# Row sums and weight sums of the third unit ordered behind the last token tile, and a Gelu given later, in the up projection of a ConvFFN

## The chip, the cores and the metric

The kernel runs on one core of one Trainium2 chip. The core has a matrix engine (PE), whose weight loads (PEld) overlap its products, and three engines for element-wise work: DVE (VectorE), ACT (ScalarE) and POOL (GpSimd). SP issues DMAs. Each of them takes its instructions from a queue of its own, in order, and waits at an instruction until what it needs is there. The metric is the time of one execution on the device in microseconds (us), smaller being better, as the median of several executions.

## The reference

A trunk of one encoder layer over 1024 tokens of width 1024: a token mixer, cross-attention into 256 memory tokens, and a gated ConvFFN, each added to its scaled input and normalised. The change lies where the cross-attention ends and the ConvFFN begins. Cut to that:

```python
def conv_ffn(h_in, w_up, b_up, w_dw, b_dw, w_down, b_down):
    h = h_in @ w_up + b_up                       # 1024 x 1024 times 1024 x 5632
    h = lax.conv_general_dilated(h, w_dw[:, None, :], ..., feature_group_count=2 * D_FF) + b_dw   # width 3 over tokens
    g, u = jnp.split(h, 2, axis=-1)              # D_FF = 2816 each
    y = jax.nn.gelu(g, approximate=False) * u
    return y @ w_down + b_down

h = layer_norm(DN_ALPHA * h + memory_xattn(h, ...), ln2_w, ln2_b)
h = layer_norm(DN_ALPHA * h + conv_ffn(h, ...), ln3_w, ln3_b)
```

## The kernel before

**Units.** The up projection is cut into 22 units (`NFF`). Unit v holds 128 columns of g and the 128 columns of u that are multiplied with them. Each unit's product with the tokens is made by a scheme with seven products instead of eight (Winograd's form of Strassen's), on quarters: weights A11, A12, A21, A22 with the sums S1 to S4, tokens B11, B12, B21, B22 with the sums T1 to T4. All operands are split into a high and a low 16-bit part, so that one product is three matmuls for each of four slices (`mm3`, lines 224 to 226), 12 matmuls of 128 x 512, and a unit has 7 x 12 = 84.

**Weights of a unit** (class `Units`, lines 1505 to 1576). `load` (L1517) brings 1 MB into one of two buffers `ur`; units 0 and 1 have buffers of their own. `bound` sums the absolute values of each row on ACT (L1524, output to the scratch tile `junk`, of which there is one) and casts the sums on DVE (L1525). `scale` sends them through PE (L182, tile `mx`) and five small steps on DVE (L183, L174 to L176, L1533) to a power of two. `sums` makes S1 to S4 on POOL (L1547 to L1550). `split_A` and `split_S` scale and split on ACT (L203) and DVE (L204). `prep` is sums, split_A and split_S as a generator with four steps. Once `split_A` and `sums` are done, the buffer `ur` is free for the next load.

**Tokens.** `out_d` ends the cross-attention for one token tile of 128 tokens: an eviction (L1480), the norm (`ln_tile`: statistics L237 and L239, L241, a power of -1/2 on POOL at L242, for the last tile the normalising step L244), the store to DRAM (L1483). `to_B` then transposes the tile on PE (L1381), evicts it on ACT (L1284) and DVE (L1286), and for every second tile forms T1 to T4 and B22 and splits them (`pair`: ACT at L1411, DVE at L1412, for some on POOL). The last tile's `to_B` runs after the products A11 B11 and A12 B21 of unit 0, which need nothing of it, are given; those of unit 1 are given behind it. Then comes `units.bound(2, junk)`.

**The loop of the up projection** (lines 1779 to 1829), for each v: load unit v+3; weight sums of unit v+2; product A11 B11 of unit v and its eviction m1 (L1709); scale of unit v+2; A12 B21 and C11; A22 T4 and C21 of unit v-1; split_A; S2 T2 and u2; the first half of `post` for unit v-2 in the order of the loop (depthwise convolution: L1683 on ACT, L1684 and L1685 on DVE); the row sum of unit v+3; S1 T1; S4 B22 and C12 of unit v-1; the split of the sums; S3 T3, u3 and C22; then the second half of `post` (Gelu L1689 on ACT, product with u L1690 on DVE, store of y L1691, its largest absolute values by a sum L1692 on ACT); and a survey of a piece of w_down (DMA L1727, row sum L1728). The PSUM bank X of a unit takes A11 B11, is evicted by m1, and takes S2 T2 on top, so PE must wait for m1 before S2 T2.

**Order.** The text gives a rank, not the order itself. When the program is built, the order of each engine's queue is worked out from simulated times: of the instructions that are ready then, the one that stands first in the text goes first (line 2001). `with tc.issue_after(x.ins):` adds an order: what is given inside the block comes behind x in the queue, where both are on the same engine. It adds no wait between engines.

Of the kernel before, what the change touches and what calls it, by code (L numbers as in the profile page):

```python
# [13 lines left out]
AF = mybir.ActivationFunctionType  # L14
OP = mybir.AluOpType
# [35 lines left out]
def run(gen):  # L51
    for _ in gen:
        pass
# [3 lines left out]
def encoder(ctx, tc, I, out):  # L57
    nc = tc.nc
    V, A, G, T, S = nc.vector, nc.scalar, nc.gpsimd, nc.tensor, nc.sync
# [19 lines left out]
    def bank(name):  # L79
        key = "mem" if name == "tk" else name  # L80
        turn[key] = turn.get(key, -1) + 1
        tag = SET[name][turn[key] % len(SET[name])]
        return pp.tile([128, 512], F32, name=name, tag=tag, bufs=NB[tag])
# [23 lines left out]
    mhalf = consts.tile([128, 4], F32, name="mhalf")  # L107
# [122 lines left out]
        V.tensor_tensor(lo, src, hi.bitcast(F32), OP.subtract)  # L230


    def ln_tile(r, w_t, b_t, small, late=False, hold=None, eps=EPS, parts=1, pieces=2):
        st = small.tile([128, pieces, 6], F32, name="lnst", tag=f"lnst{pieces}", bufs=3 if pieces == 2 else 1)
        with (tc.issue_after(hold.ins) if hold is not None else nullcontext()):
            for i in range(pieces):
                V.bn_stats(st[:, i, :], r[:, i * D // pieces:(i + 1) * D // pieces])  # L237
        mv = small.tile([128, 2], F32, name="lnmv", bufs=3)
        V.bn_aggr(mv, st)  # L239
        rs = small.tile([128, 2], F32, name="lnrs", bufs=3)  # L240
        V.tensor_scalar(rs[:, 0:1], mv[:, 1:2], eps, None, op0=OP.add)  # L241
        G.tensor_tensor(rs[:, 0:1], rs[:, 0:1], mhalf[:, 0:1], OP.pow)  # L242
        if late and w_t is None:
            return V.tensor_scalar(r, r, mv[:, 0:1], rs[:, 0:1], op0=OP.subtract, op1=OP.mult)  # L244
        if late:
            for i in range(parts):
                c = slice(i * D // parts, (i + 1) * D // parts)
                V.scalar_tensor_tensor(r[:, c], r[:, c], mv[:, 0:1], w_t[:, c], op0=OP.subtract, op1=OP.mult)
                V.scalar_tensor_tensor(r[:, c], r[:, c], rs[:, 0:1], b_t[:, c], op0=OP.mult, op1=OP.add)
            return  # L250
        n = V.tensor_scalar(rs[:, 1:2], mv[:, 0:1], rs[:, 0:1], -1.0, op0=OP.mult, op1=OP.mult)
        A.activation(r, r, AF.Identity, scale=rs[:, 0:1], bias=rs[:, 1:2])
        if w_t is None:
            return n
        a = V.tensor_tensor(r, r, w_t, OP.mult)
        G.tensor_tensor(r, r, b_t, OP.add)
        return a
# [1016 lines left out]
    with ExitStack() as cb_:  # L1274
# [26 lines left out]
        todo = [0, 2, 1, 3, 4, 6, 5, 7]  # L1301
        rs, hT, probs, rq, holds, stores = {}, {}, {}, [], [], []
# [71 lines left out]
        def to_B(r, tt):  # L1374
# [33 lines left out]
            T1, T2, T3, T4 = t12[:, 0], t12[:, 1], t34[:, 0], t34[:, 1]  # L1408
            def pair(n, src):
                h, l = (t[:, :, o] for t in Bop[n])  # L1410
                A.activation(h, src, AF.Copy)  # L1411
                (G if n in ("B22", "T3") and tt not in todo[-2:] else V).tensor_tensor(l, src, h, OP.subtract)  # L1412

            V.tensor_tensor(T1, e12, B1[:, 0], OP.subtract)
            V.tensor_tensor(T2, e22, T1, OP.subtract)
# [2 lines left out]
            V.tensor_tensor(T3, e22, e12, OP.subtract)  # L1418
            if tt not in todo[-2:]:
                pair("B22", e22)  # L1420
            pair("T3", T3)
            V.tensor_tensor(T4, B1[:, 1], T2, OP.subtract)
            pair("T4", T4)
            if tt in todo[-2:]:
                pair("B22", e22)

        Vo = [[], []]
        for i in range(4):
# [149 lines left out]
        units = Units()  # L1578
# [40 lines left out]
        junk = ur.tile([128, 2048], BF, name="junk")  # L1619

        def prod(ps, v, a, b, first, last):
            (ah, al), (bh, bl) = units.got[v][a], Bop[b]
            for k in range(4):
                mm3(ps, ah[:, k, :], al[:, k, :], bh[:, k, :], bl[:, k, :], first and k == 0, k == 3, skip=True)
# [21 lines left out]

        with rtx:

            X, Z, W = {}, {}, {}
            for v in range(2):  # L1650
                X[v], Z[v] = bank("z"), bank("z")
                if rq and v == 1:
                    to_B(*rq.pop(0))
                prod(X[v], v, "A11", "B11", True, False)
                prod(Z[v], v, "A12", "B21", True, True)
                W[v] = bank("z")
            run(units.split_S(1))
            units.bound(2, junk)

# [3 lines left out]
        with ExitStack() as cE:  # L1665
# [109 lines left out]
                sy[g] = scale_of(ysum[:, :NG] if g == 0 else ysum[:, NG:], 14)  # L1775

            take(0, "m1")
            loaded, posts = None, []
            for v in range(NFF):
                loaded = units.load(v + 3) or loaded  # L1780
                pr = units.prep(v + 2)
                next(pr, None)
                if v > 1:
                    X[v], Z[v], W[v] = bank("z"), bank("z"), bank("z")
                    prod(X[v], v, "A11", "B11", True, False)
                if v > 1:
                    take(v, "m1")
                units.scale(v + 2)
                if v > 1:
                    prod(Z[v], v, "A12", "B21", True, True)  # L1790
# [28 lines left out]
                prod(X[v], v, "S3", "T3", False, False)  # L1819
                take(v, "u3")  # L1820
                take(v, "C22")
                if posts:
                    run(posts.pop())
                if v > 0:
                    posts.append(post(v - 1))
                if v < NFF - 2:
# [2 lines left out]
                        survey_down(NFF - 1 - v // 10)  # L1829

            v = NFF - 1
            ps = {}
            w_pair(1, 0)
            for tt in range(5):
# [13 lines left out]
        with ExitStack() as cF:  # L1848
# [39 lines left out]
            rs = {}  # L1888
# [9 lines left out]
            for tt in range(NT):  # L1898
# [10 lines left out]
                n = 256 if last else 512  # L1909
# [95 lines left out]
```

## Time and profile before

| | |
|---|---|
| median of 3 executions | 1481.03 us (1478.51 to 1482.34) |
| profiled execution, its time | 1481.55 us |
| its span, first to last instruction | 1479.8 us |
| PE busy | 1435.1 us |
| mean granted clock of PE | 0.993 |
| DVE, ACT, POOL busy | 1034.1, 821.5, 553.5 us |

A row of a list in order of time has the start in us from the span's first instruction, the duration, the engine, the line of the kernel, the operation, output and inputs by tile name with their sizes, and in brackets the idle time of the engine before it with what ended it. Matmuls overlap: one of 128 x 512 lasts 0.38 us, and the next may start 0.22 us after it. A row of the stretches has the bounds, the length, and for PE, PEld, DVE, ACT and POOL the busy time with the number of instructions, then the granted clock of PE as a share of full speed, the busy share of the DMA engines and GB/s.

### The profile page before, as it was taken

Reading aid. Unit: us, or ns where it says so; the run is one execution under the profiler, and the core shown is the slowest. Engines: PE = TensorE matmul, PEld = TensorE weight load, DVE = VectorE, ACT = ScalarE, POOL = GpSimd, SP = SyncE. Lnnn points to the kernel's source line nnn. Section 1 sums busy time; section 2 is a strip of 40 time slices with the busy share of each in tenths; the row PEclk is TensorE's granted clock in tenths of the full one; section 3 lists DMA queues with packets and bytes.
Section 4 is the critical chain, followed back from the end, with each engine's and each line's share of the span. In section 5 each row is a group of like instructions: output and inputs, shape, how many; then the busy total and the mean of one; then the engine's idle time right before and its main releaser. Section 6 shows DMA issues by size and latency. Waiting matters only on the chain. (4 is left out here: it accounts for less than half of the span.)

```text
span 1479.8 us, 21506 instructions
## 1 busy us (share of the span) xinstructions
PE 1435.1 (97%) x7996; PEld 844.2 (57%) x7996; DVE 1034.1 (70%) x1950; ACT 821.5 (56%) x1385; POOL 553.5 (37%) x440
## 2 busy tenths in 40 slices
PE   8999899999999999999999899999999999999998
PEld 6998776456766777774444444444444444444445
DVE  7867866535777778589658878787888888707424
ACT  5765465565563576424455777777777767403001
POOL 4452356502334766055114153343444400300543
PEclk9999999999999999999999999999999999999999
DMA  8845654214654644643343333233322437603121
GB/s 302 318 180 198 184 190 153 84 50 129 159 147 152 206 142 141 256 148 72 86 100 86 116 143 128 114 114 128 114 114 113 144 142 242 228 28 110 47 71 58
DMA packets 116383, 208.61 MB, mean 141 GB/s; under 512 B 40627, under 2 KB 69555, under 8 KB 112950
## 3 DMA queue, kind: packets, MB, share of 16 engines
q1 hardware_dynamic: 115984, 206.47, 42.0%
q8 instruction: 63, 1.03, 0.3%
q0 software_dynamic: 144, 0.49, 0.2%
q14 instruction: 42, 0.34, 0.1%
q10 hardware_dynamic: 150, 0.27, 0.0%
HBM read 154.15 MB, written 45.15 MB: 135 GB/s over the span
## 5 line engine op out<-in xcount | busy, mean ns | idle before, releaser
L1547 POOL TENSOR_TENSOR wraw<-ur 128x512 f32<-128x512 f32 x20 | 42.5, 2125 | 213.6 <-issue 193.0
L225 PE MATMUL dn<-wlo,yp 128*128 128x512 f16 (+1 forms) x284 | 105.1, 370 | 0.0
L224 PE MATMUL dn<-whi,yp 128*128 128x512 f16 (+1 forms) x284 | 104.9, 370 | 0.0
L226 PE MATMUL dn<-whi,yp 128*128 128x512 f16 (+1 forms) x284 | 104.4, 370 | 0.0
L1684 DVE SCALAR_TENSOR_TENSOR cbuf<-C,wdw,cbuf 128x1024 f32<-128x1024 f32 x44 | 71.4, 1623 | 30.8 <-ACT cbuf L1683 30.4
L225 PEld LDWEIGHTS <-whi 128*128 128x128 f16 x540 | 52.8, 98 | 58.0 <-issue 5.9
L226 PEld LDWEIGHTS <-wlo 128*128 128x128 f16 x540 | 52.8, 98 | 56.7 <-DVE wlo L204 1.3
L224 PEld LDWEIGHTS <-whi 128*128 128x128 f16 x540 | 52.8, 98 | 54.7 <-issue 1.7
L204 DVE SCALAR_TENSOR_TENSOR wlo<-wraw,us,whi 128x1024 f16<-128x1024 f32 (+1 forms) x48 | 62.8, 1325 | 21.3 <-ACT whi L203 21.3
L242 POOL TENSOR_TENSOR lnrs<-lnrs,mhalf 128x1 f32<-128x1 f32 x32 | 23.5, 735 | 127.4 <-DVE lnrs L241 90.2
L1685 DVE SCALAR_TENSOR_TENSOR cbuf<-C,wdw,cbuf 128x1024 f32<-128x1024 f32 x44 | 69.8, 1587 | 1.1
L1683 ACT ACTIVATE cbuf<-C,bdw,wdw 128x1024 f32<-128x1024 f32 x44 | 54.4, 1235 | 17.8 <-DVE C L1721 17.2
L1524 ACT ACTIVATE junk<-ur 128x2048 bf16<-128x2048 f32 x20 | 38.2, 1912 | 40.1 <-DMA ur<-in_w_up_dram 40.1
L203 ACT ACTIVATE whi<-wraw,us 128x1024 f16<-128x1024 f32 (+1 forms) x48 | 51.1, 1102 | 16.0 <-DVE us L176 15.8
L225 PEld LDWEIGHTS <-yp 128*128 128x128 f16 x370 | 36.2, 98 | 39.9
L224 PEld LDWEIGHTS <-yp 128*128 128x128 f16 x370 | 36.2, 98 | 39.8
L226 PEld LDWEIGHTS <-yp 128*128 128x128 f16 x370 | 36.2, 98 | 39.7
L224 PE MATMUL tk<-whi,Bo 128*128 128x256 f16 (+1 forms) x192 | 52.6, 274 | 2.9 <-DVE stage L204 2.9
L224 PE MATMUL tk<-whi,Be 128*128 128x256 f16 (+1 forms) x192 | 52.6, 274 | 0.9 <-DVE stage L204 0.8
L225 PE MATMUL tk<-wlo,Be 128*128 128x256 f16 (+1 forms) x192 | 52.4, 274 | 0.8 <-DVE wlo L204 0.8
L226 PE MATMUL tk<-whi,Bo 128*128 128x256 f16 (+1 forms) x192 | 52.5, 274 | 0.0
L226 PE MATMUL tk<-whi,Be 128*128 128x256 f16 (+1 forms) x192 | 52.5, 274 | 0.0
(555 smaller groups left out, 4802.2 us busy)
## 6 DMA issues: line engine op xcount, KB each, us to landing
ur<-in_w_up_dram SPq DMA_DIRECT2D x20, 1024.0 KB
sv<-in_w_down_dram SPq DMA_DIRECT2D x22, 512.0 KB
y<-cbuf SPq DMA_DIRECT2D x22, 512.0 KB
ur<-y SPq DMA_DIRECT2D x11, 1024.0 KB
wraw<-in_w_down_dram SPq DMA_DIRECT2D x22, 512.0 KB
r<-h SPq DMA_DIRECT2D x11, 512.0 KB
wraw<-in_w_tok_dram SPq DMA_DIRECT2D x10, 512.0 KB
wr<-in_w_xk_dram SPq DMA_DIRECT2D x8, 512.0 KB
```

Source lines behind the costliest of these rows:

```text
L203: A.activation(hi, src, AF.Copy, scale=s)
L204: return V.scalar_tensor_tensor(lo, src, s, hi, op0=OP.mult, op1=OP.subtract)
L224: T.matmul(ps, lh, rh, start=first, stop=False, skip_group_check=skip)
L225: T.matmul(ps, lh, rl, start=False, stop=False, skip_group_check=skip)
L226: return T.matmul(ps, ll, rh, start=False, stop=last, skip_group_check=skip)
L242: G.tensor_tensor(rs[:, 0:1], rs[:, 0:1], mhalf[:, 0:1], OP.pow)
L1524: A.activation(junk, self.raw[v], AF.Abs, accum_out=l1)
L1547: G.tensor_tensor(S1, A21, A22, OP.add)
L1683: A.activation(c, C[:, 1:SEQ + 1], AF.Identity, scale=wdw[:, 1, j:j + 1], bias=bdw[:, j:j + 1])
L1684: V.scalar_tensor_tensor(c, C[:, 0:SEQ], wdw[:, 0, j:j + 1], c, op0=OP.mult, op1=OP.add)
L1685: V.scalar_tensor_tensor(c, C[:, 2:SEQ + 2], wdw[:, 2, j:j + 1], c, op0=OP.mult, op1=OP.add)
```

## The change

Two parts, all in order; the instructions and their operands stay as they are.

First, the power of the last token tile's norm and the two instructions that split its T3 are remembered. The row sum and cast of the third unit (v = 2) are put behind those two, and the first step of its `prep`, the four weight sums on POOL, behind the power.

Second, the second half of `post` (Gelu to the row sum of y) is no longer given at the end of a round but in the next one, behind the load, the weight sums, the first product and its eviction m1, and ahead of `scale`. After the last round it is run once more.

```diff
+    power = [None]
...
-        G.tensor_tensor(rs[:, 0:1], rs[:, 0:1], mhalf[:, 0:1], OP.pow)
+        power[0] = G.tensor_tensor(rs[:, 0:1], rs[:, 0:1], mhalf[:, 0:1], OP.pow)
...
-                A.activation(h, src, AF.Copy)
-                (G if n in ("B22", "T3") and tt not in todo[-2:] else V).tensor_tensor(l, src, h, OP.subtract)
+                a = A.activation(h, src, AF.Copy)
+                b = (G if n in ("B22", "T3") and tt not in todo[-2:] else V).tensor_tensor(l, src, h, OP.subtract)
+                return a, b
...
-            pair("T3", T3)
+            ends = pair("T3", T3)
...
+            return ends
...
+            powered = power[0]
...
-                    to_B(*rq.pop(0))
+                    ends = to_B(*rq.pop(0))
...
-            units.bound(2, junk)
+            with tc.issue_after(ends[0].ins), tc.issue_after(ends[1].ins):
+                units.bound(2, junk)
...
-            loaded, posts = None, []
+            loaded, posts, ending = None, [], ()
...
-                next(pr, None)
+                with (tc.issue_after(powered.ins) if v == 0 else nullcontext()):
+                    next(pr, None)
...
                     take(v, "m1")
+                run(ending)
                 units.scale(v + 2)
...
-                if posts:
-                    run(posts.pop())
+                ending = posts.pop() if posts else ()
                 if v > 0:
                     posts.append(post(v - 1))
...
             v = NFF - 1
+            run(ending)
```

## The prediction

> **What bounds the kernel now.** First the page's busy line, then busy time by stretch, then the waits of PE from the start of the up projection on: a row says who waited for whom, us in total, how often, the longest.
>
> ```profile
> PE 1435.1 (97%) x7996; PEld 844.2 (57%) x7996; DVE 1034.1 (70%) x1950; ACT 821.5 (56%) x1385; POOL 553.5 (37%) x440
> ```
> ```profile
> 838.00:849.00 11.00, 6.43 (x23) 2.37 (x22) 11.00 (x28) 9.44 (x17) 0.00 (x0) 0.84 0.19 54
> ...
> 1003.00:1155.00 152.00, 148.73 (x691) 67.05 (x690) 122.59 (x141) 113.25 (x132) 63.14 (x32) 1.00 0.30 115
> ```
> ```profile
> 1200.00:1250.00 50.00, 50.00 (x236) 23.08 (x234) 46.55 (x54) 36.46 (x39) 0.00 (x0) 1.00 0.62 211
> ```
> ```profile
> PE z L224 <- ACT C L1709: 3.3, 8, 0.9
> PE z L224 <- ACT C L1713: 1.6, 3, 0.8
> ...
> PE z L225 <- DVE TX1l L1412: 0.6, 1, 0.6
> PE mx L182 <- DVE am L1525: 0.4, 1, 0.4
> ```
>
> PE is busy 97% of the span, so a change pays only where PE stands still. Two places of the up projection matter. Between 838 and 849 us PE is busy for 6.43 of 11.00 us and its clock falls to a mean of 0.84: 4.57 us idle. Later it loses 3.3 us in eight short waits for L1709, the first eviction of a unit ("m1"). From 1200 us on it is full, so time won earlier should reach the end.
>
> The order of PE through the first place:
>
> ```profile
> 835.85 1.06 PE L1381 MATMUL tp<-ident,r 128*128 128x128 f32 x8
> ...
> 838.26 0.38 PE L226 MATMUL z<-Bh,unitA 128*128 128x512 f16 x1
> 839.67 0.22 PE L182 MATMUL mx<-identb,am 128*128 128x128 bf16 x1 [1.03 <-ACT spare L1284]
> 841.43 0.22 PE L182 MATMUL mx<-identb,am 128*128 128x128 bf16 x1 [1.54 <-DVE us L183]
> ...
> 844.91 0.58 PE L225 MATMUL z<-TX1l,unitYh 128*128 128x512 f16 x1 [0.65 <-DVE TX1l L1412]
> ...
> 847.40 0.38 PE L225 MATMUL z<-TX1l,unitYh 128*128 128x512 f16 x1
> ...
> 848.27 0.38 PE L226 MATMUL z<-TX1l,unitYh 128*128 128x512 f16 x1
> ```
>
> At 835.85 come the transposes of the last token tile, at 838.26 the last product that needs none of it, and only at 844.91 do the products on the sums T1 to T4 run on. Behind the stall six matmuls take 847.40 - 844.91 = 2.49 us, 0.415 each, the next four (848.27 - 847.40) / 4 = 0.22 each: 6 x 0.195 = 1.2 us lost to a half clock. Loss: 4.57 + 1.2 = 5.8 us, and about 5 x (0.38 - 0.22) = 0.8 us more, since a broken row of matmuls counts each last one at its full 0.38: 6.6 us.
>
> **Why the last tile is late.** DVE, POOL and ACT:
>
> ```profile
> 808.50 0.21 DVE L241 TENSOR_SCALAR lnrs<-lnmv,sc 128x1 f32<-128x1 f32 x1
> 809.38 0.21 DVE L251 TENSOR_SCALAR lnrs<-lnmv,lnrs 128x1 f32<-128x1 f32 x1 [0.66 <-POOL lnrs L242]
> ...
> 827.83 0.21 DVE L239 BATCH_NORM_AGGREGATE lnmv<-lnst 128x2 f32<-128x12 f32 x1
> 830.72 0.16 DVE L1525 CAST am<-l 128x1 bf16<-128x1 f32 x1 [2.69 <-ACT junk L1524]
> 830.79 0.20 DVE L241 TENSOR_SCALAR lnrs<-lnmv,sc 128x1 f32<-128x1 f32 x1
> ...
> 833.67 2.04 DVE L244 TENSOR_SCALAR r<-r,lnmv,lnrs 128x1024 f32<-128x1024 f32 x1
> ...
> 844.18 0.68 DVE L1412 TENSOR_TENSOR TX1l<-spare,TX1l 128x512 f16<-128x512 f32 x1
> ```
> ```profile
> 828.82 1.28 POOL L1547 TENSOR_TENSOR wraw<-ur 128x512 f32<-128x512 f32 x1 [8.85 <-DMA ur<-in_w_up_dram]
> ...
> 832.52 1.00 POOL L242 TENSOR_TENSOR lnrs<-lnrs,mhalf 128x1 f32<-128x1 f32 x1
> 833.48 1.27 POOL L1550 TENSOR_TENSOR wraw<-ur,wraw 128x512 f32<-128x512 f32 x1
> ```
> ```profile
> 828.69 1.91 ACT L1524 ACTIVATE junk<-ur 128x2048 bf16<-128x2048 f32 x1 [4.07 <-DMA ur<-in_w_up_dram]
> ...
> 832.65 1.93 ACT L1524 ACTIVATE junk<-ur 128x2048 bf16<-128x2048 f32 x1
> ...
> 843.51 0.63 ACT L1411 ACTIVATE TX1l<-spare 128x512 f16<-128x512 f32 x1
> ...
> 846.16 1.58 ACT L203 ACTIVATE unitYl<-ur,us 128x1536 f16<-128x1536 f32 x1
> ```
>
> Each engine works off its queue in order. ACT stands 4.07 us before the third unit's row sum (L1524, 828.69), which waits for a DMA, while evictions of the last token tile but one lie behind it. DVE stands 2.69 us at the cast L1525 that waits for the same row sum, with L241 of the last tile's norm behind it. On POOL the power L242 lies behind three weight sums of the third unit and starts only at 832.52. So the norm's last step L244 starts at 833.67, though its statistics were ready at 828.04.
>
> **The change, first part.** The two edges put unit 2's row sum (ACT) and cast (DVE) behind the last tile's T3 split, and its first weight sums (POOL) behind the last power; unit 3's row sum writes the same tile junk and stays behind. No instruction is added or left out. Queued behind the moved ones are, on ACT, the T4 split and the weight splits; on DVE, the steps from scale product to scale; on POOL, the clearing of the C buffers' edges, which the first convolution reads long after.
>
> Norm: 828.04 plus the 0.88 us that another tile shows from L241 through POOL to the next DVE step (808.50 to 809.38) is 828.9, not 833.67: 4.75 us earlier. The transposes can then run about 831 instead of 835.85, and in front of them ACT has lost the 4.07 us stand and two row sums (1.91 and 1.93). From the end of the transposes (835.85 + 1.06 = 836.9) to the end of the first T split needed (844.18 + 0.68 = 844.9) passed 8.0 us. Kept at 8.0 it ends at 840; PE has products until 838.5, so 1.5 us of stall is left. Shortened by what no longer lies in it, none is. PE wins 6.6 - 1.5 = 5.1 at least, 6.6 at most if the order of PE uses the earlier tile; I take 6.2, nearer the upper end, because ACT's 1.2 us (836.9 to the tile's evictions at about 838.1) and the two scale products mx both leave that stretch.
>
> What is late next: unit 2's weights. T3's split on ACT ended at 843.51 + 0.63 = 844.14; 6 us earlier it is 838.1. Behind it come two row sums, 2.1 us each with their read of the sum (1.91 + 0.19), then the split of unit 2 (L203): 842.3 instead of 846.16, 3.9 us earlier. It frees the buffer for unit 4's load, and the two rows of buffers make unit 5's load, row sum and scale product wait in turn. That product already held PE up:
>
> ```profile
> 866.55 0.23 PE L182 MATMUL mx<-identb,am 128*128 128x128 bf16 x1 [0.37 <-DVE am L1525]
> ```
>
> PE, 6.2 us earlier, meets a weight chain that is only 3.9 earlier, with no slack there: it gives back 2.3 us. Bounds for this term: nothing, if the scale product is placed later in PE's queue, and all but the chain's own gain. First part: 6.2 - 2.3 = 3.9 us, between 0 and 6.6, and below 0 by the rival named slower.
>
> **Second part.** The Gelu, its product, the store of y and the row sum L1692 are given after the next unit's load, weight sums, first product and m1, and after the survey row sum L1728. Instructions stay the same; SP gets the weight load ahead of the store of y, which costs nothing, as the load waits for its buffer and not for the queue. One of the eight rounds:
>
> ```profile
> 1038.38 0.76 ACT L1715 ACTIVATE C<-z,bup,us 128x512 f32<-128x512 f32 x1
> 1041.15 1.06 ACT L1689 ACTIVATE cbuf<-cbuf 128x1024 f32<-128x1024 f32 x1 [2.01 <-DVE cbuf L1685]
> 1042.11 0.77 ACT L1709 ACTIVATE C<-z,bup,us 128x512 f32<-128x512 f32 x1
> ```
> ```profile
> 1031.93 0.38 PE L226 MATMUL z<-Bh,wlo 128*128 128x512 f16 x1
> 1032.14 0.38 PE L224 MATMUL z<-TX1l,unitYl 128*128 128x512 f16 x1
> ...
> 1034.73 0.38 PE L224 MATMUL z<-Bh,whi 128*128 128x512 f16 x1
> ...
> 1036.46 0.38 PE L226 MATMUL z<-Bh,wlo 128*128 128x512 f16 x1
> ...
> 1042.93 0.38 PE L224 MATMUL z<-TX1h,whi 128*128 128x512 f16 x1 [0.42 <-ACT C L1709]
> ```
> ```profile
>   DVE cbuf L1685: 32.2, 17
> ```
>
> The last row is ACT's idle time before Gelu: 32.2 us in 17 rounds. Here m1 could run from 1036.8 on, but lies behind Gelu, which stands 2.01 us for the convolution; PE waits 0.42. With m1 in front it runs at 1039.1 in that idle time and the wait is gone: 3.3 us over the eight rounds is the most. The other bound is nothing: who comes first is settled when the program is built, by what is ready then (PE takes three products of the next unit, leaves them at 1032.14 for the earlier unit's, and returns at 1034.73). In these rounds Gelu may thus lead because it was ready first in that reckoning, and a later place in the text need not turn that; then this part does not do what it says. Below nothing it goes only where m1, put in front, holds Gelu up: its product ends at 1036.8, 4.3 us before Gelu can start (1041.15), so not here. I take a third of the upper bound, 1.1 us, as the reckoning is not to be seen in the trace and one row speaks for each side.
>
> **Sum.** 3.9 + 1.1 = 5.0 us off the span of 1479.8: 1474.8. Around the span lie 1481.55 - 1479.8 = 1.75 us, and the profiled execution is 0.5 above the median of 1481.03: 1474.8 + 1.75 - 0.5 = 1476.0 us.
>
> **Rivals.**
>
> *Both parts in full* (0.18): the scale products fall where they cost nothing and m1 leads in all eight rounds: 6.6 + 3.3 = 9.9, 1471.1 us. For it: after each Gelu the next split then comes at once, which shortens the weight chain too. Against it: unit 5's product had no slack.
>
> *The weight chain swallows it* (0.20): the chain, not PE, sets the pace (Gelu, split, load, row sum, convolution, Gelu; from 1003 to 1155 us PE idles 3.27 us on it), and what PE wins at 849 it waits out later. With a chain only 0 to 2 us earlier: 1479 to 1481.
>
> *POOL blocks DVE* (0.10). L244 took 2.04 us where POOL's L1550 ran until 833.48 + 1.27 = 834.75; another step of its kind and size took 0.74:
>
> ```profile
> L1859 DVE TENSOR_SCALAR vec<-vec,sc x1: 741/741/741, 1220.7 to 1220.7; 128x1024 f32<-128x1024 f32 x1
> ```
>
> 834.75 to L244's end at 835.71 is 0.96, so it stood for about 1.1. Four weight sums now start right behind the power, at the very time of L244 and of the sums T1 to T4. One or two blocks of 1.3 us on the last tile's path leave 1477 to 1478.5. The Trainium skill, SBUF — State Buffer, section "Who interferes with whom", states such a lock: DVE's two-port modes share a port pair with GpSimd, and whichever issues first holds the other off for its whole instruction. By that rule this rival comes true at least once; the trace agrees with the lock (2.04 against 0.74).
>
> *Slower* (0.10): third unit late. If the last tile comes earlier by a, the split of unit 2 starts at 844.14 - a + 4.2 = 848.3 - a against 846.16. Below a = 2.2 us the chain is later than before, and each later unit with it, through the buffers. At a = 0, an order on PE that keeps the transposes where they were and scale products that hold PE, this is 2.2 us and up to 2 x 2.1 us for PE at the two scale products: 1481 + 2.2 to 6.4 = 1483 to 1487.
>
> **How the numbers follow.** Forecast 0.42 (1474 to 1478.5 alone), the rivals 0.18, 0.20, 0.10, 0.10. Range 1471 to 1483: it leaves out the lower half of the full case and most of the slower one. The measurement of this kernel can tell 0.3%, 4.4 us: faster means under 1476.6. From the forecast 0.29, from the full case 0.18: 0.47; slower 0.07 from the slower case and a reshuffled order; same 0.46.
>
> **What would show it.** Norm: L244 starts near 829 to 830 and the transposes before 833. Stall: PE's idle time between the last Bh product of unit 1 and steady T products under 1.5 us, the clock at 1.00. Chain: split of unit 2 (L203) at 842 to 843, and a wait of PE for L1525 of about 2 us near 860. Second part: L1709 in front of L1689 in the rounds around 1003 to 1155, PE's waits for L1709 below 3.3 us. The prediction is wrong if PE's queue keeps the scale products ahead of the T products, if the Gelu order is turned everywhere, or if a later stage turns out to lack the slack that its full PE suggests.

## The result, and the profile after

| | before | after |
|---|---|---|
| median of 10 executions each | 1481.43 us (1478.46 to 1484.69) | 1486.71 us (1482.88 to 1488.42) |
| profiled execution, its span | 1479.8 us | 1486.1 us |
| first product of the up projection to the first of the down projection | 409.34 us | 415.32 us |

The changed kernel is slower: ratio 1.0041 [1.0029, 1.0053]. The forecast was 1476.0 us with a range from 1471 to 1483; sign and range were both wrong.

The third row comes from the starts of two matmuls in the list of PE in order of time, for before (1236.33 - 826.99) and for after (1242.55 - 827.23):

```profile
826.99 0.38 PE L224 MATMUL z<-Bh,unitYh 128*128 128x512 f16 x1
...
1236.33 0.38 PE L224 MATMUL dn<-whi,yp 128*128 128x512 f16 x1
```
```profile
827.23 0.38 PE L224 MATMUL z<-Bh,unitYh 128*128 128x512 f16 x1
...
1242.55 0.38 PE L224 MATMUL dn<-whi,yp 128*128 128x512 f16 x1
```

Behind it lie 243.5 us in both, so all that was lost (5.98 us in these two executions) was lost in the up projection. Where that projection starts differs by up to 4.3 us between the profiled executions of this study; times of different kernels are therefore compared from its first product on.

Lines of the changed kernel are numbered 2 to 6 higher: L246 is the norm's last step, L1413 and L1414 are the splits of `pair`, L1417 to L1425 the sums T1 to T4, L1286 and L1288 the evictions of a transposed tile, L1528 and L1529 row sum and cast, L1551 to L1554 the weight sums, L1715, L1719, L1721 and L1725 the evictions m1, u2, u3 and C21. First the stretch of the old stall, then the waits of PE from 826 to 1180 us, in the changed kernel, and behind them one row of the same waits in the kernel before:

```profile
838.00:849.00 11.00, 7.19 (x27) 2.66 (x26) 8.80 (x17) 10.16 (x18) 0.00 (x0) 0.84 0.25 77
```
```profile
PE z L224 <- ACT C L1715: 4.6, 11, 1.5
PE z L224 <- ACT TX1l L1413: 3.7, 1, 3.7
PE z L224 <- ACT C L1721: 3.4, 2, 2.7
PE z L224 <- ACT C L1725: 1.5, 1, 1.5
PE z L224 <- ACT C L1719: 1.1, 1, 1.1
PE z L224 <- DVE C L1723: 1.1, 1, 1.1
```
```profile
PE z L224 <- ACT C L1715: 0.9, 2, 0.6
```

The stall is still there: 3.81 us idle instead of 4.57, the clock at 0.84 as before, now in one piece of 3.7 us instead of several. New are the waits for C21 (L1725) and C22 (L1723). The waits for u3 (L1721, L1715 before) have grown from 0.9 to 3.4 us and those for m1 from 3.3 to 4.6 us. Those for u2 (L1719, L1713 before) have shrunk from 1.6 to 1.1 us, but lie at another place, behind unit 2's split.

PE's idle time plus what the half clock cost (each interval between two starts above 0.25 us, less 0.216, the interval at full clock), in us from the first product of the up projection:

| stretch | before | after |
|---|---|---|
| 0 to 30 us, with the old stall | 4.63 + 1.20 | 4.83 + 0.76 |
| 30 to 110 us | 1.74 + 0.07 | 5.27 + 1.75 |
| 110 us to the end | 4.42 + 0.27 | 5.27 + 0.21 |

The sums are 12.3 and 18.1 us; their difference, 5.8 us, is the 5.98 us that were lost, within 0.2 us. Of the 4.83 us in the first row, 1.10 us are the wait for u2 at 856.24; at the old stall itself PE lost 3.73 + 0.76 us, 1.3 us less than before. So there are two questions: why the first stretch won next to nothing, and what lost 5.2 us in the second.

**The first stretch.** DVE, POOL, ACT and PE of the changed kernel:

```profile
829.71 1.75 DVE L246 TENSOR_SCALAR r<-r,lnmv,lnrs 128x1024 f32<-128x1024 f32 x1 [0.44 <-POOL lnrs L244]
...
833.06 1.75 DVE L1418 TENSOR_TENSOR ysum<-r,ysum 128x512 f32<-128x512 f32 x1
834.74 1.76 DVE L1421 TENSOR_TENSOR ysum<-r 128x512 f32<-128x512 f32 x1
```
```profile
829.65 1.26 POOL L1551 TENSOR_TENSOR wraw<-ur 128x512 f32<-128x512 f32 x1
830.88 1.71 POOL L1553 TENSOR_TENSOR wraw<-ur 128x512 f32<-128x512 f32 x1
...
834.34 1.60 POOL L1554 TENSOR_TENSOR wraw<-ur,wraw 128x512 f32<-128x512 f32 x1
```
```profile
832.20 0.63 ACT L1413 ACTIVATE whi<-r 128x512 f16<-128x512 f32 x1 [2.27 <-DVE r L1288]
834.85 0.63 ACT L1413 ACTIVATE TX1h<-ysum 128x512 f16<-128x512 f32 x1 [2.02 <-DVE ysum L1418]
...
838.27 2.18 ACT L1286 ACTIVATE spare<-tp,wb 128x128 f32<-128x128 f32 x6
...
843.20 0.66 ACT L1413 ACTIVATE TX1l<-spare 128x512 f16<-128x512 f32 x1
...
851.87 1.57 ACT L203 ACTIVATE unitYl<-ur,us 128x1536 f16<-128x1536 f32 x1
```
```profile
834.14 1.04 PE L1383 MATMUL tp<-ident,r 128*128 128x128 f32 x8
...
842.36 0.58 PE L224 MATMUL z<-TX1l,unitYh 128*128 128x512 f16 x1 [3.73 <-ACT TX1l L1413]
...
850.72 0.22 PE L182 MATMUL mx<-identb,am 128*128 128x128 bf16 x1
...
856.24 0.38 PE L224 MATMUL z<-TX1l,unitYh 128*128 128x512 f16 x1 [1.10 <-ACT C L1719]
```

The norm starts at 829.71, some 4 us earlier than before, as forecast. But the four weight sums now start with it, and while they run, the norm takes 1.75 us, and so do two of DVE's sums for tile 6, T2 and T3, instead of 0.68 each. (Tile 6 is the last token tile but one.) ACT splits tile 6 in front of the last tile's evictions and waits for DVE four times: 2.27 us for an eviction of DVE's (L1288) that stands behind the norm, 2.02 us for T2, and less for T3 and T4. The transposes of the last tile come at 834.14 without a wait: PE's queue has them behind other products. The last tile's evictions thus begin at 838.27 (838.13 before), and the split of T3 at 843.20 (843.51 before): not 6 us earlier but 0.3. The row sum of the third unit follows it, its scale product stands in PE's queue behind products of the last tile and runs at 850.72 without any wait of PE, and unit 2's split starts at 851.87 instead of 846.16. Behind that split stands the eviction u2, for which PE waits at 856.24.

**The second stretch.** SP, ACT, DVE and PE of the changed kernel, and behind it SP and ACT of the kernel before:

```profile
855.53 0.33 SPq L1521 DMA_DIRECT2D ur<-in_w_up_dram  x1
...
864.33 0.33 SPq L1521 DMA_DIRECT2D ur<-in_w_up_dram  x1
```
```profile
871.45 1.91 ACT L1528 ACTIVATE junk<-ur 128x2048 bf16<-128x2048 f32 x1 [4.55 <-DMA ur<-in_w_up_dram]
...
873.35 0.76 ACT L1725 ACTIVATE C<-z,bup,us 128x512 f32<-128x512 f32 x1
...
882.45 1.56 ACT L203 ACTIVATE unitYh<-ur,us 128x1536 f16<-128x1536 f32 x1
...
897.14 1.06 ACT L1695 ACTIVATE cbuf<-cbuf 128x1024 f32<-128x1024 f32 x1 [2.67 <-DVE cbuf L1691]
898.11 1.56 ACT L203 ACTIVATE unitA<-ur,us 128x1536 f16<-128x1536 f32 x1
...
901.65 0.77 ACT L1721 ACTIVATE C<-z,bup,us 128x512 f32<-128x512 f32 x1
```
```profile
873.48 0.16 DVE L1529 CAST am<-l 128x1 bf16<-128x1 f32 x1 [4.86 <-ACT junk L1528]
```
```profile
902.47 0.38 PE L224 MATMUL z<-TX1h,unitYl 128*128 128x512 f16 x1 [2.68 <-ACT C L1721]
...
903.66 0.63 PE L226 MATMUL z<-TX1h,unitYl 128*128 128x512 f16 x1
```
```profile
850.08 0.33 SPq L1517 DMA_DIRECT2D ur<-in_w_up_dram  x1
...
859.09 0.33 SPq L1517 DMA_DIRECT2D ur<-in_w_up_dram  x1
```
```profile
864.30 1.91 ACT L1524 ACTIVATE junk<-ur 128x2048 bf16<-128x2048 f32 x1 [1.18 <-DMA ur<-in_w_up_dram]
...
871.05 1.56 ACT L203 ACTIVATE unitYh<-ur,us 128x1536 f16<-128x1536 f32 x1
```

The loads of units 4 and 5 are issued 5.4 and 5.2 us later, since they wait for buffers. The row sum of unit 5 stands in ACT's queue in front of C21, so ACT stands 4.55 us (1.18 before) and DVE, at the cast, 4.86; PE waits for C21. Unit 4's split slips from 871.05 to 882.45. Near 897 Gelu waits 2.67 us for the convolution, three splits follow, and only then comes u3, for which PE stands 2.68 us; the 0.63 us at 903.66 is the half clock behind it.

**The second part** of the change did nothing. Up to their line numbers, the instructions of all five engines stand in the same order in the kernel before and in the kernel before with this part alone (run 1).

### The profile page after: what moved, and what is told of

It is laid out like the page before. It is cut to its first block, busy times and chain, and to the rows that moved or that the text cites. A ratio compares the mean times of both kernels' runs of the same rounds, so it can differ in the third digit from the quotient of the medians.

```text
span 1486.1 us, 21505 instructions
## 1 busy us (share of the span) xinstructions
PE 1439.8 (97%) x7996; PEld 846.8 (57%) x7996; DVE 1041.1 (70%) x1950; ACT 821.7 (55%) x1385; POOL 558.2 (38%) x440
## 4 chain that ended last, share of the span: by engine, by line
PE 61%; DVE 13%; DMA 9%; ACT 9%; issue 4%; POOL 2%; SPq 1%; DVEq 0%; ACTq 0%; POOLq 0%
DMA ur<-in_w_up_dram 5%; PE dn L225 5%; PE dn L226 5%; PE dn L224 5%; PE S L224 4%; PE S L225 4%; PE S L226 4%; PE tk L224 2%; PE tk L225 2%; PE tk L226 2%; DVE cbuf L1690 2%; DVE cbuf L1691 2%; PE cl L224 2%; PE cl L225 2%; PE cl L226 2%
## 5 line engine op out<-in xcount | busy, mean ns | idle before, releaser
L1551 POOL TENSOR_TENSOR wraw<-ur 128x512 f32<-128x512 f32 x20 | 40.7, 2036 | 208.3 <-issue 172.2
L1528 ACT ACTIVATE junk<-ur 128x2048 bf16<-128x2048 f32 x20 | 38.3, 1913 | 37.7 <-DMA ur<-in_w_up_dram 37.6
L225 PE MATMUL tk<-wlo,Bo 128*128 128x256 f16 (+1 forms) x192 | 53.7, 280 | 0.0
L224 PE MATMUL tk<-whi,Be 128*128 128x256 f16 (+1 forms) x192 | 52.6, 274 | 0.1
```

The source lines that it names most:

```text
L224: T.matmul(ps, lh, rh, start=first, stop=False, skip_group_check=skip)
L225: T.matmul(ps, lh, rl, start=False, stop=False, skip_group_check=skip)
L1528: A.activation(junk, self.raw[v], AF.Abs, accum_out=l1)
L1551: G.tensor_tensor(S1, A21, A22, OP.add)
```

## The experiments

Ratios are to the kernel before, with their 95% intervals. The last column is the length from the first product of the up projection to the first of the down projection in the one profiled execution, 409.34 us for the kernel before; it need not agree with the ratio, which is of medians.

| run | ratio | us |
|---|---|---|
| the change | 1.0041 [1.0029, 1.0053] | 415.32 |
| 1 second part alone | 1.0002 [0.9993, 1.0011] | 409.83 |
| 2 row sum and cast late, POOL as before | 1.0018 [1.0009, 1.0027] | 412.32 |
| 3 weight sums behind the power, row sum as before | 1.0012 [1.0003, 1.0022] | 412.60 |
| 4 row sum early, weight sums behind the power | 1.0002 [0.9994, 1.0011] | 411.43 |
| 5 row sum late, weight sums behind tile 6's T4 | 1.0047 [1.0035, 1.0058] | 413.86 |
| 6 row sum early, weight sums behind tile 6's T4 | 1.0014 [1.0006, 1.0023] | 410.92 |
| 7 kernel before, third unit's load not held back | 1.0036 [1.0024, 1.0047] | 412.13 |
| 8 kernel before, unit 2's split held back | 1.0005 [0.9994, 1.0015] | 410.70 |
| 9 row sum early, weight sums behind the last T4 | 1.0010 [0.9999, 1.0021] | 410.95 |
| 10 row sum late, weight sums behind the last T4 | 1.0024 [1.0015, 1.0033] | 412.24 |
| 11 row sum early, POOL as before | 1.0004 [0.9994, 1.0014] | 409.63 |
| 12 the change, unit 5's row sum put back | 1.0009 [0.9996, 1.0022] | 410.71 |
| 13 kernel before, unit 5's row sum put back | 1.0001 [0.9988, 1.0013] | 410.78 |
| 14 run 10, unit 5's row sum put back | 0.9990 [0.9978, 1.0003] | 409.51 |
| 15 run 9, unit 5's row sum put back | 0.9992 [0.9977, 1.0006] | 408.48 |

**Taking the change apart: runs 1 to 3.** Run 1 is the second part alone, run 2 the edges on ACT and DVE alone, run 3 the edge on POOL alone, each in the kernel before:

```diff
-                if posts:
-                    run(posts.pop())
+                ending = posts.pop() if posts else ()
...
+                run(ending)
                 units.scale(v + 2)
```
```diff
-            units.bound(2, junk)
+            with tc.issue_after(ends[0].ins), tc.issue_after(ends[1].ins):
+                units.bound(2, junk)
```
```diff
-                next(pr, None)
+                with (tc.issue_after(powered.ins) if v == 0 else nullcontext()):
+                    next(pr, None)
```

> The second part alone (Gelu half of post given a round later in the text; no edge on the row sums or weight sums). Theory A (the third unit's row sums come too late behind the T3 split, so its weight split, and every later load through the two buffers, slips by 5 to 6 us) and theory B (POOL's weight sums, now at the same time as the last tile's DVE steps, block them): both expect no change, 1481.4 within 2 us, the Gelu still ahead of m1 in the later rounds and PE's waits for m1 at 3.3 us. Theory C (the Gelu's new place is what costs): 1485 to 1488, most of the loss.

> Only the edges on the row sum and the cast of the third unit; the weight sums on POOL stay ahead of the power, Gelu as before. Theory A: slower by 4 to 7 us (1485 to 1488), the first split of unit 2 on ACT near 852 instead of 846.2. Theory B: within 2 us of before, since POOL's sums lie where they lay. Theory C: as before.

> Only the edge of the weight sums behind the power on POOL. Theory A: not slower, 1478 to 1482, as the row sums stay early and unit 2's split at 846 or before. Theory B: slower by 3 to 6 us (1484 to 1487), with DVE's steps L244, T2 and T3 of the last tiles at 1.7 us instead of 0.7. Theory C: as before.

The second part is out: level. Each half of the first part is a loss, 0.18% and 0.12%, both smaller than the theories expected (2.7 us for 4 to 7, 1.8 us for 3 to 6). Run 2 has the new waits 30 to 110 us after the start (2.59 us and a half clock of 1.68); run 3 has none there (0.20 us) but loses 9.2 us instead of 5.8 in the first stretch.

**Early places: runs 4 and 11.** The row sum is put only behind tile 6's last eviction on ACT, the cast behind the last norm. Run 4 keeps the edge on POOL, run 11 leaves it out.

```diff
+        normed = holds[-1]
         to_B(*rq.pop(0))
+        evicted6 = evicted[0]
...
-            with tc.issue_after(ends[0].ins), tc.issue_after(ends[1].ins):
+            with tc.issue_after(evicted6.ins), tc.issue_after(normed.ins):
                 units.bound(2, junk)
```

> The first part with its edges moved forward: the third unit's row sum behind the last ACT eviction of the last token tile but one (not behind the T3 split), its cast behind the last tile's normalising step, the weight sums behind the power as in the change; Gelu as before. Theory A: the loss is gone; the row sums fill ACT's idle time between 829 and 838, unit 2's split starts at 846 or before, 1476 to 1481. Theory B: the weight sums collide as in the changed kernel, so still slower than before by 3 to 6 us.

> Row sum and cast in the early place (behind tile 6's last eviction on ACT and behind the last norm), the weight sums on POOL without an order of their own, so that they may run ahead of the last power as in the kernel before. Theory: the norm of the last tile is late as before (832 to 833), the sums T1 to T4 run without POOL beside them but the evictions of tile 6 no longer wait for the third unit's load; unit 2's split at 846 to 848. Level with the kernel before: 0.999 to 1.001. If the order of POOL was a loss by itself in the early place, this run is faster than that one by 1 to 2 us.

Both are level, neither is faster. With the row sum early, the second stretch is like that of before (1.37 and 0.87 us lost). The new waits thus come with the late row sum, but the runs do not yet say by what.

**Without POOL beside tile 6: runs 5 and 6.** A small copy on POOL reads tile 6's T4 (`summed`) and the weight sums come behind it. Run 5 keeps the late row sum, run 6 has the early one.

```diff
+            summed[0] = T4[:, 0, 0:1]
...
-            powered = power[0]
+            held = small.tile([128, 1], F32, name="held")
+            with tc.issue_after(power[0].ins):
+                powered = G.tensor_copy(held, summed[0])
```

> The first part of the change with one small POOL copy more, which reads the last sum T4 of the last token tile but one and stands between the power and the weight sums: the sums start some 6 us later, after DVE's steps of that tile. Theory B (POOL's weight sums hold DVE up on the path): DVE's normalising step falls from 1.75 to about 0.75 us and T2 and T3 of that tile from 1.75 to 0.7, the evictions of the last tile on ACT start at 835 to 836 instead of 838.3, the split of unit 2 near 849 instead of 851.9, and 2 to 4 of the 6 us come back: 1482 to 1484. If the lock only fills time that the ACT queue would lose anyway: no change, 1486 to 1488.

> Row sum and cast of the third unit moved forward as in the run before (behind the last tile but one's evictions and the normalising step) and the small POOL copy ahead of the weight sums. Theories A and B together: both costs are gone, the last tile's evictions start before 835, PE's stall before the T products falls from 4.6 us to 1 to 3 us, 1475 to 1479, faster than before. If something else holds the last tile: 1480 to 1482, like the run without the copy.

In run 5 the sums of tile 6 take 0.7 us, and the last tile's evictions start at 834.4; but the weight sums now lie beside the last tile's own sums, which take 1.0 to 1.8 us, and nothing is won. POOL's hold (its weight sums lengthening DVE's steps) had only been moved by one tile. Run 6, expected to be faster, is slower by 0.14%: it has no new waits in the second stretch (0.49 us), but loses 7.5 us in the first.

**The load instead of the row sum: run 7.** The kernel before without the order that keeps the third unit's load behind the last store of h.

```diff
-        with tc.issue_after(stores[-1].ins):
-            units.load(2)
+        units.load(2)
```

> The kernel before, without the edge that puts the third unit's load behind the store of the last token tile but one; nothing of the change. Both loads then leave SP some 10 us earlier and the row sum, the cast and the weight sums find their data without waiting. If the wait for this load is the root of the stall at 838: ACT's 4.07 us and DVE's 2.69 us are gone, the normalising step starts near 829, PE's stall shrinks by 2 to 4 us, 1476 to 1479. If the stores behind the loads or the DMA engines then hold the tiles up: 1481 or more.

Slower: PE then stands 2.19 and 1.72 us at the transposes of the last two tiles.

**Is a late unit a loss by itself? Run 8.** Three more row sums, results unused, are put behind the last tile's B22 split and ahead of unit 2's split in the kernel before.

```diff
-                pair("B22", e22)
+                ends = pair("B22", e22)
...
+                more = nullcontext()
+                if v == 0:
+                    for k in range(3):
+                        with tc.issue_after(ends[0].ins):
+                            last = A.activation(junk, units.raw[2], AF.Abs, accum_out=small.tile([128, 1], F32, name="more", tag="more", bufs=3))
+                    more = tc.issue_after(last.ins)
-                next(pr, None)
+                with more:
+                    next(pr, None)
```

> The kernel before, with three more row sums of unit 2's weights on ACT (1.9 us each, results unused) between the last split of the last token tile and unit 2's split; nothing else is moved. They put unit 2's split at about 852 us instead of 846.2, as the change does, while the token chain, the weight sums and the products stay as in the kernel before. Late unit (theory): the lateness alone costs most of what the change costs, 3 to 6 us, 1.002 to 1.004, and PE shows new waits for the first evictions of units 2 and 3 between 856 and 905 us. Stall and lock (rival: the change costs what it does by the wait of PE for the last tile's sums, 3.7 us at 842, and by POOL's hold on DVE): the later units have slack and this kernel is level with the one before, 1.000 to 1.001.

ACT and SP of this run:

```profile
854.07 1.58 ACT L203 ACTIVATE unitYl<-ur,us 128x1536 f16<-128x1536 f32 x1
...
870.05 1.91 ACT L1528 ACTIVATE junk<-ur 128x2048 bf16<-128x2048 f32 x1
```
```profile
858.01 0.33 SPq L1521 DMA_DIRECT2D ur<-in_w_up_dram  x1
```

Unit 2's split starts 7.9 us later than before, and the load of unit 4 is issued 7.9 us later: more than in the changed kernel. Yet the run is level, with 1.01 us lost in the second stretch. The theory that I held until then, that the late split is what costs, fell here. What differs: the row sum of unit 5 has no bracket at 870.05. It is behind m1 in ACT's queue (ahead of it in the kernel before), and ACT does not stand at it. By the load of unit 6 the lateness is nearly gone: 877.52, against 875.56 before and 885.93 in the changed kernel. The run is not the late split alone, though. As built, one of the row sums stands ahead of three of the last tile's splits, and the first stretch loses 8.0 us instead of 5.8.

**The weight sums behind the last tile: runs 9 and 10.** The copy reads the last tile's T4 instead of tile 6's. Row sum early in run 9, late in run 10.

```diff
-            powered = power[0]
...
+            with tc.issue_after(power[0].ins):
+                powered = G.tensor_copy(held, summed[0])
             run(units.split_S(1))
```

> Row sum and cast of the third unit behind tile 6's last eviction on ACT and behind the last norm (as in the run with the early place), and its four weight sums on POOL behind a copy that reads the last tile's T4, so that none lies beside the norm or the sums T1 to T4 of either tile. Theory: the early place keeps unit 2's split at 845 to 847, and without the hold on DVE the last tile's sums come 3 to 5 us earlier than with POOL beside them; the weight sums end about 850, before the split's last piece frees the buffer, and cost nothing. Level with the kernel before to faster by 3 us: 0.998 to 1.000. If the hold on DVE was not what kept the early place from winning, it is level with that run, 1.000 to 1.001. If late weight sums hold the load of unit 4, it is slower, 1.001 to 1.003.

> The changed kernel's row sum and cast of the third unit (behind the last tile's T3 split), the weight sums on POOL behind the same copy of the last tile's T4 as in the run before this one, the Gelu as before. No weight sum lies beside the token chain, so what is left of the change is the late row sum. Theory (late unit): unit 2's split lies at 850 or later, the kernel is slower than the one before by 2 to 5 us, 1.0015 to 1.0035, and slower than the run with the early place by as much. Rival (the hold on DVE carries the loss): level with the kernel before, 1.000 to 1.001.

Run 10 is the late row sum without POOL beside the norm and the sums of either tile. It is still a loss, with 4.83 us of PE's waits in the second stretch (mostly for u3 and C22, none for C21 near 871) and a stand of ACT, 2.59 us, at unit 5's row sum. Run 9 missed its expectation: it lost 4.4 us in the first stretch instead of 5.8 and gave 3.8 us back at one wait at 886 us, which follows a stand of 2.6 us at the same row sum.

**The stand: runs 12 and 13.** One order more, in the changed kernel and in the kernel before: unit 5's row sum behind unit 2's m1 on ACT, its cast behind unit 4's scale on DVE.

```diff
-                    take(v, "m1")
+                    m1 = take(v, "m1")
...
-                units.bound(v + 3, junk)
+                with (tc.issue_after(m1.ins) if v == 2 else nullcontext()), (tc.issue_after(units.scaled.ins) if v == 2 else nullcontext()):
+                    units.bound(v + 3, junk)
```

> The changed kernel with one more order: the row sum of unit 5 behind unit 2's eviction m1 on ACT, its cast behind the scale of unit 4 on DVE. In the changed kernel these two stand first in line when the weights of unit 5 land late: ACT idles 4.55 us and DVE 4.9 us there, with the eviction C21 of unit 1, the scale of unit 4 and the first convolutions behind them; unit 4's split then falls behind the second Gelu, the load of unit 6 comes 10 us late and PE loses 1.52 us at 874 and 2.68 us and a half clock at 902. Theory (the stand in line is the cost, not the lateness itself): C21 runs at 869 to 870, the wait of PE at 874 is gone, the load of unit 6 is at 876 to 880, the wait at 902 and its half clock go, and the kernel is 3 to 5 us faster than the changed one: 1.0005 to 1.002 of the kernel before. Rival (a later weight chain costs by itself, wherever the row sums stand): 1.003 to 1.0045 as in the changed kernel.

> The kernel before with the one order of the last experiment: the row sum of unit 5 behind unit 2's eviction m1 on ACT, its cast behind the scale of unit 4 on DVE. In the kernel before ACT stands only 1.2 us at that row sum. Theory (the order mends what the change broke): level, 0.999 to 1.001. Rival (the order is a gain in any kernel): 0.9965 to 0.998, as it was worth 0.3% in the changed kernel.

Run 12, the waits of PE for C in the same stretch as above, and ACT:

```profile
PE z L224 <- ACT C L1715: 5.1, 11, 1.5
...
PE z L224 <- ACT C L1721: 2.4, 2, 1.9
```
```profile
863.80 0.76 ACT L1725 ACTIVATE C<-z,bup,us 128x512 f32<-128x512 f32 x1
...
872.34 1.90 ACT L1528 ACTIVATE junk<-ur 128x2048 bf16<-128x2048 f32 x1
...
876.87 1.58 ACT L203 ACTIVATE unitYh<-ur,us 128x1536 f16<-128x1536 f32 x1
...
892.75 0.77 ACT L1721 ACTIVATE C<-z,bup,us 128x512 f32<-128x512 f32 x1
893.41 1.56 ACT L203 ACTIVATE unitA<-ur,us 128x1536 f16<-128x1536 f32 x1
```

Its first product starts 3.2 us earlier than in the profiled execution of the changed kernel (824.02 against 827.23). On that kernel's clock C21 runs at 867.0 instead of 873.35, and the row sum has no stand. (ACT stands 3.79 us at a survey row sum instead, at 868.36, with convolutions and m1 behind it, and PE waits for nothing there.) PE's waits for C21 and C22 are gone, its longest wait for u3 is 1.9 us instead of 2.7, and there is no half clock behind it: the second stretch loses 1.89 us instead of 7.02. The intervals of the change and of this run, [1.0029, 1.0053] and [0.9996, 1.0022], do not overlap. In the kernel before the same order is worth nothing (run 13), so it mends something that the change broke. Two points of the expectation were missed: unit 4's split is only 2.4 us earlier on the changed kernel's clock (876.87 + 3.2 = 880.1), some 9 us later than in the kernel before, and the load of unit 6 comes at 883.6 on that clock, not at 876 to 880. The weight chain is still late.

The one order also turned others when the queues were built: about 20 instructions on ACT and 60 on PE stand elsewhere. One of them is u3, which is ahead of the three splits in run 12 (892.75) and behind them in the changed kernel (901.65). The wait at C21, 1.52 us, lies right behind the stand; that the waits for u3 and C22 and the half clock come from the stand, and not from u3's place in the queue, is not shown.

**Both mended: runs 14 and 15.** Runs 10 and 9 with that order.

> The changed kernel's late row sum of the third unit, the weight sums on POOL behind the last tile's T4, the Gelu as before, and the order for unit 5's row sum. Neither POOL beside the token chain nor a stand at unit 5's row sum is left of the change. Theory: 1.0000 to 1.0010 of the kernel before, some 2 us less than the same kernel without that order (1.0024). If a late third unit costs by itself, 1.002 or more.

> The row sum of the third unit in the early place, the weight sums on POOL behind the last tile's T4, and the order for unit 5's row sum. Its form without that order lost 4.4 us at the first stall and after it instead of 5.8, and gave back 3.8 us by one wait of PE at 886 us with a half clock behind it, which followed a stand of ACT and DVE of 2.6 us at unit 5's row sum. Theory: the stand goes, and the kernel is 1 to 4 us faster than the kernel before: 0.9975 to 0.9995. If the time simply turns up in another wait of the same chain, 1.000 to 1.001.

DVE and ACT of run 14:

```profile
827.51 0.92 DVE L246 TENSOR_SCALAR r<-r,lnmv,lnrs 128x1024 f32<-128x1024 f32 x1 [0.44 <-POOL lnrs L244]
...
829.59 0.68 DVE L1418 TENSOR_TENSOR ysum<-r,ysum 128x512 f32<-128x512 f32 x1
...
838.10 1.44 DVE L1414 TENSOR_TENSOR TX1l<-spare,TX1l 128x512 f16<-128x512 f32 x1
```
```profile
832.64 2.19 ACT L1286 ACTIVATE spare<-tp,wb 128x128 f32<-128x128 f32 x6
...
837.58 0.66 ACT L1413 ACTIVATE TX1l<-spare 128x512 f16<-128x512 f32 x1
...
848.81 1.56 ACT L203 ACTIVATE unitYl<-ur,us 128x1536 f16<-128x1536 f32 x1
```

The row sum is as late as in the change, behind T3's split, but without POOL beside the norm and the sums that split comes 12.56 us after the first product (837.58 - 825.02), against 16.52 before (843.51 - 826.99): the token chain is 4.0 us earlier. Unit 2's split is 23.8 us after the first product, 4.6 later than before, and the kernel is level. With run 8 that is the second kernel in which a late third unit is no loss in all.

PE won less than the chain did. At the old stall run 14 still loses 2.0 us and 1.7 to a half clock (4.57 and 1.2 before). The hold had moved once more: the weight sums now lie beside the last tile's low splits, the first of which takes 1.44 us instead of 0.68 (838.10), and PE waits 1.2 us for it. Then PE waits 0.4 us for unit 2's split and 1.1 us for the u2 behind it, so the late unit is not free at its own split.

The change and runs 10, 12 and 14 form a square of two factors: the weight sums beside the norm and tile 6 (the hold), and unit 5's row sum ahead of m1 (the stand, with the order that was built around it). The ratio is 1.0041 with both, 1.0024 with the stand alone, 1.0009 with the hold alone, 0.9990 with neither. The second factor is worth 0.0032 and 0.0034 (some 4.9 us; 4.6 and 2.7 us in the profiled executions), and in both pairs the intervals are apart. The hold is worth 0.0017 and 0.0019 (some 2.7 us; 3.1 and 1.2 us in the profiled executions); there each pair's intervals overlap, and only that both pairs agree speaks for the size. This factor is a clean one: between the change and run 10, and between runs 12 and 14, the instructions of PE, DVE and ACT stand in the same order, and only POOL's differ. (Runs 10 and 14 have the Gelu as before and one small copy on POOL more; run 1 says that the first does not matter.) Run 14 lies below its expectation and run 15 within it, but neither beats the kernel before by more than its interval.

What stays open, beside u3's place: why the built order puts unit 5's row sum where it does in the changed kernel. The simulated times that it rests on are not in the trace, which shows only that the weights landed later than that place allows for.

## Why the prediction was wrong

1. **Norm and power: right.** L246 starts at 829.71, within the 829 to 830 given. It lasts 1.75 us (0.92 in run 14, without weight sums beside it): the rival that POOL blocks DVE came true.
2. **The last tile's chain 6 us earlier: the step that failed.** "Kept at 8.0 it ends at 840" took the distance from the transposes to the T splits before as an upper bound. It grew: from the end of the transposes (834.14 + 1.04 = 835.2) to the first low T split's end (843.72 + 0.68 = 844.4) it is 9.2 us. In it now lie tile 6's splits on ACT, which wait for steps of DVE that POOL's weight sums hold up. The transposes themselves, expected about 831 and before 833, came at 834.14, because PE's queue had them behind other products. The block had its place among the rivals, priced at one or two blocks of 1.3 us, with a chance of 0.10; it was not in the main sum, although the change moves exactly those four sums there. The Trainium skill, SBUF — State Buffer, section "Who interferes with whom", states the case more broadly than the prediction used it: a DVE instruction with two SBUF inputs also contends with GpSimd's reads. The trace agrees: the sums T2 and T3 take 1.75 us beside weight sums and 0.68 without. With the weight sums behind T4 the T3 split is 4.0 us earlier, not 6, and the low splits are then blocked (run 14).
3. **PE wins 6.2 us at the stall: it won 1.3** (5.8 us lost there before, 4.5 after), for the reason in 2. A new wait of 1.1 us for u2, behind unit 2's late split, takes most of that back, so the first 30 us won 0.2.
4. **Unit 2's split at 842 to 843: it is at 851.87.** The working by the rival "slower" held better: with a = 0.3 it gives 848.0. The rest is PE's queue: the scale product stands behind products of the last tile, where the prediction took the old distance from row sum to split.
5. **The give-back of 2.3 us at the scale product near 860: wrong place, too small.** The scale products made PE wait nowhere. PE waited for C21, which stands in ACT's queue behind work that waits for late weights, and for u3 and C22; the second stretch lost 5.2 us more than before. The prediction followed the weight chain to PE through its own products and not through the queue of ACT, although it had read the same thing in the kernel before: ACT standing 4.07 us before a row sum with evictions behind it. In the changed kernel the stand is at unit 5's row sum, 4.55 us (1.18 before).
6. **Second part, 1.1 us: nothing.** "Then this part does not do what it says" was the case.
7. **The rival "slower"** had the right condition (a below 2.2 us) and a price that holds the result (1483 to 1487; 1486.71 measured), but not its carrier: in runs 8 and 14 a later third unit was level with the kernel before; the loss went with the order of unit 5's row sum and with the hold. Its chance of 0.10 and the range's upper end of 1483 were too low, because the norm's gain was taken to reach the T splits.

## What to carry to other kernels

An instruction that is put later to clear one path meets others there: before POOL work is moved, list what DVE does at its new time, and price each two-input step at its measured blocked length (here 1.75 for 0.68 us). A wait in an in-order queue is priced by what stands behind it, so when a load gets later, look for every consumer of it that stands ahead of evictions; a late chain with nothing behind it may cost nothing. And a later place in the program text is no later place in the queue where the order is worked out at build: compare the order of the instructions first.

## What the runs showed of the hardware that was not expected

The hold between POOL and DVE slows both: beside each other the weight sums take 1.71 us (830.88 in the changed kernel) instead of the 1.26 to 1.28 of the kernel before, and DVE's sums 1.75 instead of 0.68, so that four weight sums in a row stretch the norm and the two or three sums beside them.

A single wait of PE of little more than 2 us can halve its clock, and does not always. In run 9 a wait of 2.09 us was followed by matmuls at intervals of 0.43 us, at a mean granted clock of 0.51 until 889.30, 1.68 us lost:

```profile
885.84 0.57 PE L224 MATMUL z<-TX1l,unitYl 128*128 128x512 f16 x1 [2.09 <-ACT C L1724]
...
887.06 0.63 PE L224 MATMUL z<-TX1l,unitYl 128*128 128x512 f16 x1
```

In run 10 waits of 2.17, 2.33 and 2.10 us were followed by none: the granted clock stayed at 1.00. Waits of up to 1.9 us that stood alone in a full stream were never followed by a half clock in these runs.
